# Halves of q and k brought into place by DMAs, weight loads issued from GpSimd, constants second in the queue

## The chip, the cores and the metric

The kernel runs on one core of one Trainium2 chip. The metric is the device time of one execution in microseconds (us), measured over several runs of which the median is given. Beside it stands one execution that was recorded by the hardware profiler; its span runs from the first to the last instruction. The engines are called TensorE (PE in the rows, its weight load PEld), VectorE (DVE), ScalarE (ACT), GpSimd (POOL) and SyncE (SP). The last one only issues DMAs here.

## The reference

The reference is a decoder trunk of two layers over 512 tokens of width 1024, all in float32. Each layer normalises its input, multiplies it by one wide projection, and feeds two branches:

```python
h = rmsnorm(x, norm_g)
aq, ak, av, az, bqk, bv, bi, bf, bo, bz, ga, gb = split(h @ w_in)
# (A) differential attention, 8 heads with two maps of 64 each
q = rope(rmsnorm(two_map_heads(aq), q_norm_g), cos, sin)      # the same for k
p = softmax(causal(q k^T / 8));  a = p[map 0] - lam * p[map 1]
ya = (rmsnorm(a v, attn_norm_g) * (1 - lam_init) * silu(az)) @ w_out_a
# (B) mLSTM, 8 heads, a matrix memory in stabilised form
mq, mk = split(silu(causal_conv(bqk, conv_w, conv_b)))
hb = mlstm(mq, mk, bv, bi + igate_b, bf + fgate_b)
yb = (sigmoid(bo) * rmsnorm(hb, mlstm_norm_g) * silu(bz)) @ w_out_b
x = x + (sigmoid(ga) * ya + sigmoid(gb) * yb) @ w_o
```

## The kernel before

**Precision.** TensorE is fed float32r values. A float32 operand is split in two: hi is the operand rounded to float32r (a cast), lo is the operand less hi (a subtraction). A product of two split operands takes three matmuls: hi by hi, hi by lo, lo by hi. The helper `split(hi, lo, src)` does the cast on ScalarE and the subtraction on VectorE.

**Pieces.** All weights are cut into pieces of 128 x 1024 (512 KB), 104 per layer beside the small gate piece. Each piece goes through the raw tile wr (two buffers) by a DMA, then is split into wh and wl (three buffers each), and then serves 24 matmuls of 512 columns. `TUNE["order"]` gives the order of the pieces; qk0 to qk3 are the four column groups of the attention's q and k, bqk0 to bqk7 those of the mLSTM's q and k.

**The order of the work.** The kernel's program is first recorded as a list of operations, by a class `Recorder`. Deferred steps (transposes of q and k, steps of each head) are put between the pieces at offsets given in `TUNE`. Then `schedule` plans all operations on a clock of its own, with a cost for each operation (`cost`), latencies between engines, a price per transferred byte, and waits for buffers. Each engine gets a fixed order by planned time; `issue` writes it out. On the chip every engine works through its own order and waits where an input or a buffer is late. SyncE and GpSimd have such orders too.

**q and k of the attention.** For each column group c and each tile of 128 tokens tt, `back` transposes four blocks into one PSUM tile qkt (pool tag "tr", one buffer, which the attention's transposed probabilities ut and the sums msp and den use in turn). A head pair's two maps lie in the rows 0 to 63 and 64 to 127. The destinations are 128 rows high: for q, hi in one half of the rows and lo in the other; for k, hi in both halves; for kl, lo in one half and zeros (a memset on GpSimd, `half_zero`) in the other. So one matmul with 128 rows does hi by hi and lo by hi together, and a second one hi by lo. In before, `back` fills them straight from PSUM: for each half of the rows three casts on ScalarE and two subtractions on VectorE, ten instructions of 64 x 256.

**q and k of the mLSTM.** `bqk_done` makes the convolution in y, applies silu, and fills mq, mql and mk in the same way from y: four casts and two subtractions of 64 x 512 for a q block, two and two for a k block.

**DMAs.** All DMAs are issued from SyncE: weight pieces, the rows that are spread over partitions for the mLSTM's decay (dd, em), the residual (xr, x1d), the output. `TUNE["start"]` is the order of the first loads: x0 to x3 (token tiles of the input), ng (the norm's weights), ct (constants, with the identity that transposes need), w0 and w1 (the first two weight pieces).

**Sums over partitions.** A mean of squares over the 128 rows is a matmul with ones. Unfolded, it takes hi and lo, two matmuls. For the heads in foldA, foldM and foldD the upper 64 rows are first added to the lower 64, and hi and lo are put into one tile (`fold`): one matmul.

Of the kernel before, what the change touches and what calls it, by code (L numbers as in the profile page):

```python
# [9 lines left out]
F32 = mybir.dt.float32  # L10
# [25 lines left out]

TUNE = {
    "order": (
# [4 lines left out]
    ),  # L43
    "qkt": 4,
    "gct": 15,
    "gls": 8,
    "glf": 11,
    "attn": (1, 5, 5, 9, 9, 9, 13, 16, 16, 19, 24),
    "a0": 23,
    "ap": 18,  # L50
    "a4": 8,
    "ml": (5, 9, 11, 12, 14, 28),
    "ahead": 3,
    "lc": 0,
    "slack": 4130.0,
    "margin": 200.0,
    "pemargin": 0.0,
    "wait": 308.1,
    "swpen": 11707.1,
    "smargin": 29.5,  # L60
    "pwait": 1.8,
    "wdiff": 9600.0,
    "wsp": 3,
    "kact": (0, 1, 2),
    "qsq": (1, 3),
    "foldA": (2, 3, 5, 6, 7),
    "foldM": (0, 1, 2, 3, 4, 5, 7),
    "foldD": (0, 1, 3, 4, 5, 6, 7),
    "warm": 18,
    "start": 'x0 ng w0 x1 ct w1 x2 x3',  # L70
    "gateA": 7,
    "gateM": 0,
    "actp": (2, 3),
    "m0": 218,
    "mp": 15,
    "m4": 20,
    "slots": 20,
    "bias": {'gi': 9700.0, 'ob': -1150.0, 'qkt': -1600.0, 'den': -1950.0, 'rq': -6100.0, 'gw': -3200.0, 'bo': -950.0, 'woa': -2700.0, 'mql': -2550.0, 'bz': -4700.0, 'av': 8250.0, 'msp_a': -2200.0, 'wl': -600.0, 'qk1_0x': -4100.0, 'hl': 16650.0, 'wh': -1350.0, 'qk': -2250.0, 'dd': -450.0, 'pb': -8050.0, 'ga': -1600.0, 'cv': -2050.0, 'cosv': -3250.0, 'az': -2000.0, 'ua': 3200.0, 'ang': -600.0, 'posf': -5750.0, 'gt': 10650.0, 'ut': 18200.0, 'fb_b': -200.0, 'num': -4050.0, 'sc': 26850.0, 'uh': -1250.0, 'msl_a': 3900.0, 'fb_d': -7600.0, 'rn': 5200.0, 'eps': 1400.0, 'bv': 1150.0, 'qk1_2x': -450.0, 'sinv': 3950.0, 'ks': 1650.0, 'wob': 2350.0, 'msh_d': -4100.0, 'fb_a': 2100.0, 'ul': -900.0, 'ml': -2100.0, 'gcol': -1300.0, 'ss': 6050.0, 'ms_b': -1150.0, 'ld': 8050.0, 'fo_d': 4250.0, 'em': 150.0, 'gf': -700.0, 'msl_b': -2800.0, 'kl': -250.0, 'qk0_0x': -950.0, 'xn': -150.0, 'ct': 3800.0, 'sbz': 3700.0, 'sums': 1300.0, 'rot': 6450.0, 'qss': -650.0, 'wo': -3700.0, 'lneps': 2450.0, 'hh': -2250.0, 'qt': 50.0, 'taz': 4700.0, 'par': 400.0, 'qs': 4900.0, 'fo_b': 1650.0, 'out_0_dram': -100.0, 'msl_d': -250.0, 'msp_b': 300.0, 'junk': 150.0, 'zw': -4200.0, 'mk': 1600.0, 'gft': 3600.0, 'gct': 1350.0, 'ms_a': 3750.0, 'rows': 2800.0, 'woh': -4650.0, 'warm': -3850.0, 'sbo': 500.0, 'mx': -3750.0, 'ms': 550.0, 'wr': -350.0, 'msh_b': -50.0, 'glf': 4000.0, 'bqk': 250.0, 'fo_a': 500.0, 'x': -2250.0, 'qy': 100.0, 'epsc': 1150.0, 'lq': 50.0, 'sdl': 1350.0, 'gm': 200.0},
    "drain": 173.2,
    "risk": 226.0,  # L80
    "late": 580.2,
}


# [16 lines left out]
class Recorder:  # L101
# [111 lines left out]
    @staticmethod  # L213
    def cost(eng, fn, a, k):
        def cols(ap):
            n = 1
            for x in list(ap.shape)[1:]:
                n *= x
            return n

        def ps(ap):
            return isinstance(ap, bass.AP) and ap.space == PSUM

        n = cols(a[0])
# [35 lines left out]
    def schedule(self):  # L260
# [65 lines left out]
        while len(order) < n:  # L326
# [51 lines left out]
                    load = table  # L378
            free[e] = s + c
            end[i] = s + c  # L380
            if e == "SP":
# [4 lines left out]
                dma = max(dma, s) + size / (175.0 if src.space != DRAM or src.tensor.name.startswith("rows") else 360.0)  # L386
                end[i] = max(dma, s) + 2000.0
            for t in o["tiles"]:
                r = rings[t["ring"]]
                if not t["live"]:  # L390
# [42 lines left out]
def kernel(ctx, tc, x, pos, wp, wg, cst, par, pb, ngb, out):  # L433
# [181 lines left out]
    def layer_events(l):  # L615
        lam_init = 0.8 - 0.6 * math.exp(-0.3 * l)
        par_l = pt[l]
        st = {}
# [205 lines left out]
        def qk_back(c, tt, rq):  # L824
# [8 lines left out]
            def back():  # L833
                pst = ps_tr.tile([P, 4, P], F32, tag="tr", name=f"qkt{l}_{c}_{tt}")
                for g in range(4):
                    T.transpose(pst[:, g, :], rq[:, g * P : (g + 1) * P], ident)
                ts = slice(tt * P, (tt + 1) * P)
                q0, q1, k0, k1 = (t[:, :, ts] for t in st[("qs", c)])
                kl0, kl1 = (t[:, :, ts] for t in st[("kl", c)])
# [101 lines left out]
        def bqk_done(m, acc):  # L941
# [439 lines left out]
    def load(i):  # L1381
# [2 lines left out]
        l, key = pieces[i]  # L1384
        w = wpool.tile([P, 1024], F32, tag="raw", bufs=2, name=f"wr{i}")
        if key == "gate":
            SY.dma_start(w[:, :512], wg[l])
        else:
            SY.dma_start(w, wp[l, KIDX[key]])
        loaded[i] = w  # L1390

    def prep(i):
# [131 lines left out]
```

## Time and profile before

| | |
|---|---|
| median of 3 runs (lowest to highest) | 1351.06 us (1350.99 to 1351.32) |
| the profiled execution, its span | 1351.41 us, 1349.6 us |
| TensorE busy, matmuls | 1338.7 us, 6364 |
| VectorE busy, instructions | 990.2 us, 1966 |
| ScalarE busy, instructions | 881.7 us, 1800 |
| GpSimd busy, instructions | 23.0 us, 28 |
| moved by DMAs | 137.68 MB, mean 102 GB/s |

The busy time of TensorE is modelled from pipelined matmuls, so "busy" is not the same as full use. In the rows below, a group of instructions is named by what it writes and reads, as wl<-wr,wh; then come the tile's partitions x elements, the count, the busy time and the mean ns of one, and the idle time of the engine before them with what ended it. A row of waits says who waited for whom, how long in total, how often, and the longest.

### The profile page before, as it was taken

To read this page: it belongs to the slowest core of one execution; us is meant where nothing else is said; L and a number is where in the kernel's file an instruction comes from. 1 tells how busy PE (TensorE), PEld (TensorE's weight loads), DVE (VectorE), ACT (ScalarE), POOL (GpSimd) and SP (SyncE) were. 2 spreads that over 40 slices of the span, in tenths; PEclk is the share of its full clock that TensorE was granted. 3 is DMA by queue.
4 is the path that set the end of the run, shared out by engine and by line. 5 is a ranking of instruction groups with operands and counts; after the bars stand their busy time and mean duration, and the time that the engine had idled before them with its cause. 6 is when DMAs were issued, how large, how long until landed. Compare 5 with 4: busy or idle time off the path is not lost. (4 is left out here: it accounts for less than half of the span.)

```text
span 1349.6 us, 17968 instructions
## 1 busy us (share of the span) xinstructions
PE 1338.7 (99%) x6364; PEld 1108.6 (82%) x6364; DVE 990.2 (73%) x1966; ACT 881.7 (65%) x1800; POOL 23.0 (2%) x28
## 2 busy tenths in 40 slices
PE   9999999999999999999999999999999999999998
PEld 7788888888888888888888888888888888888887
DVE  7888988785477877844568889888755778787452
ACT  6768978876356867833357788788753577677230
POOL 1000010000000000000000000000000000000000
PEclk9999999999999999999999999999999999999999
DMA  5323222323343433433622222221333534434332
GB/s 178 94 64 94 76 66 63 94 79 98 94 124 118 133 114 119 146 95 101 200 65 78 66 77 79 78 78 64 96 111 94 129 112 126 122 109 145 104 111 86
DMA packets 48394, 137.68 MB, mean 102 GB/s; under 512 B 5776, under 2 KB 12560, under 8 KB 48304
## 3 DMA queue, kind: packets, MB, share of 16 engines
q1 hardware_dynamic: 48304, 136.54, 33.2%
q8 instruction: 50, 0.82, 0.2%
q14 instruction: 40, 0.33, 0.1%
HBM read 132.25 MB, written 4.26 MB: 101 GB/s over the span
## 5 line engine op out<-in xcount | busy, mean ns | idle before, releaser
L429 DVE TENSOR_TENSOR wl<-wr,wh 128x512 fp32r<-128x512 f32 x400 | 264.7, 686 | 117.5 <-ACT wh L429 115.3
L429 ACT CAST wh<-wr 128x1024 fp32r<-128x1024 f32 (+1 forms) x202 | 210.8, 1045 | 207.1 <-PE wob L429 40.3
L429 PE MATMUL qk<-wl,hh 128*128 128x512 f32 x256 | 93.7, 402 | 0.0
L429 PE MATMUL qk<-wh,hl 128*128 128x512 f32 x256 | 93.7, 402 | 0.0
L429 PE MATMUL qk<-wh,hh 128*128 128x512 f32 x256 | 92.8, 401 | 0.2 <-ACT hh L429 0.2
L429 PE MATMUL woa<-oa,wh 128*128 128x512 f32 x256 | 87.7, 390 | 0.0
L429 PE MATMUL wob<-ob,wh 128*128 128x512 f32 x256 | 86.7, 389 | 0.0
L429 ACT ACTIVATE p<-sc,mx,rq 128x128 f32<-128x128 f32 (+3 forms) x128 | 78.6, 616 | 9.3 <-DVE mx L429 8.2
L428 ACT ACT_TABLE_LOAD x61 | 78.3, 1283 | 1.0
L429 PEld LDWEIGHTS wob<-ob,wh 128*128 128x128 f32 x256 | 47.9, 188 | 10.4 <-ACT sgb L429 0.2
L429 PEld LDWEIGHTS qk<-wl,hh 128*128 128x128 f32 x256 | 47.6, 188 | 10.4 <-DVE wl L429 0.9
L429 PEld LDWEIGHTS qk<-wh,hh 128*128 128x128 f32 x256 | 47.8, 188 | 10.0 <-ACT hh L429 0.5
L429 PEld LDWEIGHTS woa<-oa,wh 128*128 128x128 f32 x256 | 47.9, 188 | 9.6
L429 PEld LDWEIGHTS qk<-wh,hl 128*128 128x128 f32 x256 | 47.4, 188 | 9.4 <-DVE hl L429 0.4
L429 DVE TENSOR_REDUCE mx<-sc 128x2 f32<-128x256 f32 (+1 forms) x64 | 52.2, 816 | 0.4
L429 PE MATMUL bqk<-hh,wl 128*128 128x512 f32 x128 | 50.6, 395 | 0.0
L429 PE MATMUL bqk<-hl,wh 128*128 128x512 f32 x128 | 50.3, 393 | 0.0
L429 PE MATMUL bqk<-hh,wh 128*128 128x512 f32 x128 | 50.1, 392 | 0.0
L429 PE MATMUL ga<-hh,wl 128*128 128x512 f32 x128 | 49.7, 396 | 0.0
L429 PE MATMUL bo<-hh,wl 128*128 128x512 f32 x128 | 49.7, 393 | 0.0
L429 PE MATMUL ga<-hl,wh 128*128 128x512 f32 x128 | 49.4, 396 | 0.0
L429 PE MATMUL bo<-hh,wh 128*128 128x512 f32 x128 | 49.3, 393 | 0.0
(285 smaller groups left out, 3678.9 us busy)
## 6 DMA issues: line engine op xcount, KB each, us to landing
wr<-in_wp_dram SPq DMA_DIRECT2D x208, 512.0 KB, 3.5
dd<-rows SPq DMA_DIRECT2D x16, 256.0 KB, 3.9
em<-rows SPq DMA_DIRECT2D x16, 256.0 KB, 3.8
dd<-rows SPq DMA_DIRECT2D x16, 192.0 KB, 5.1
x<-in_x_dram SPq DMA_DIRECT2D x4, 512.0 KB, 4.8
dd<-rows SPq DMA_DIRECT2D x16, 128.0 KB, 6.3
xr<-in_x_dram SPq DMA_DIRECT2D x8, 256.0 KB, 4.1
x1d<-xn SPq DMA_DIRECT2D x8, 256.0 KB, 3.5
```

The lines of the kernel that those rows point to most:

```text
L428: self.tc.keep_in_program_order(self.nc.scalar.preload_act_table_set(self.SET_NAME[o["load"]]))
L429: self.tc.keep_in_program_order(getattr(o["e"], o["fn"])(*o["a"], **o["k"]))
```

## The change

The order of pieces and the numbers in `TUNE` that place and weigh operations are new throughout. The ones that change what is computed by whom are shown. `back` and `bqk_done` now split the whole 128-row block once, into two tiles h and l of the pool s2, and SyncE's DMAs bring the 64-row halves to their places: ten DMAs of 64 KB in `back`, six of 128 KB for a q block of the mLSTM and four for a k block. Weight pieces are loaded by DMAs that GpSimd issues. From the fourth piece on (`i < TUNE["wsp"]`), wl is made by one subtraction instead of two. The planner prices a DMA issue at 0.4 us on SyncE and 1 us on GpSimd, where it had 0.06 for SyncE.

```diff
-    "attn": (1, 5, 5, 9, 9, 9, 13, 16, 16, 19, 24),
+    "attn": (1, 5, 5, 8, 8, 10, 13, 16, 16, 19, 26),
-    "ahead": 3,
+    "ahead": 5,
-    "pemargin": 0.0,
+    "pemargin": 398.8,
-    "kact": (0, 1, 2),
-    "qsq": (1, 3),
-    "foldA": (2, 3, 5, 6, 7),
-    "foldM": (0, 1, 2, 3, 4, 5, 7),
-    "foldD": (0, 1, 3, 4, 5, 6, 7),
+    "kact": (0, 1),
+    "qsq": (1,),
+    "foldA": (0, 2, 3, 4, 5, 7),
+    "foldM": (0, 1, 2, 3, 4, 5, 6),
+    "foldD": (0, 1, 2, 3, 4, 5, 6, 7),
-    "start": 'x0 ng w0 x1 ct w1 x2 x3',
+    "start": 'x0 ct ng w0 x1 w1 x2 x3',
-    "actp": (2, 3),
+    "actp": (0, 3),
...
-            return 200.0 + n
+            return 1000.0 if fn == "dma_start" else 200.0 + n
...
-        return 60.0
+        return 400.0
...
+                go = s + c if e == "POOL" else s
+                dma = max(dma, go) + size / (175.0 if src.space != DRAM or src.tensor.name.startswith("rows") else 360.0)
+                end[i] = max(dma, go) + 2000.0
...
+    def halves(src, name):
+        hi, lo = t2(f"h_{name}", F32R), t2(f"l_{name}", F32R)
+        split(hi, lo, src)
+        return hi.bitcast(F32), lo.bitcast(F32)
...
+                h4, l4 = halves(pst.rearrange("p a b -> p (a b)"), f"qk{l}_{c}_{tt}")
                 for q, k, kl, a, b in ((q0, k0, kl0, L, H), (q1, k1, kl1, H, L)):
-                    A.copy(q[a], pst[a, 0:2, :])
-                    V.tensor_tensor(q[b], pst[a, 0:2, :], q[a].bitcast(F32), ALU.subtract)
-                    A.copy(k[a], pst[a, 2:4, :])
-                    A.copy(k[b], pst[a, 2:4, :])
-                    V.tensor_tensor(kl[a], pst[a, 2:4, :], k[a].bitcast(F32), ALU.subtract)
+                    SY.dma_start(q[a], h4[a, 0:2])
+                    SY.dma_start(k[a], h4[a, 2:4])
+                    SY.dma_start(k[b], h4[a, 2:4])
+                    SY.dma_start(q[b], l4[a, 0:2])
+                    SY.dma_start(kl[a], l4[a, 2:4])
...
+            hi, lo = halves(y, f"m{l}_{m}")
-                    A.copy(q[a, i, :], y[a])
-                    A.copy(q[b, i, :], y[a])
-                    V.tensor_tensor(st[("mql", grp)][i][a, pl, :], y[a], q[a, i, :].bitcast(F32), ALU.subtract)
+                    SY.dma_start(q[a, i, :].bitcast(F32), hi[a])
+                    SY.dma_start(q[b, i, :].bitcast(F32), hi[a])
+                    SY.dma_start(st[("mql", grp)][i][a, pl, :].bitcast(F32), lo[a])
...
-                    A.copy(k[a, i, :], y[a])
-                    V.tensor_tensor(k[b, i, :], y[a], k[a, i, :].bitcast(F32), ALU.subtract)
+                    SY.dma_start(k[a, i, :].bitcast(F32), hi[a])
+                    SY.dma_start(k[b, i, :].bitcast(F32), lo[a])
...
-            SY.dma_start(w, wp[l, KIDX[key]])
+            G.dma_start(w, wp[l, KIDX[key]])
...
-        if TUNE["wsp"]:
+        if i < TUNE["wsp"]:
```

More of the change, by code (lines that the diff above doesn't have):

```diff
@@ L45 @@
     "gct": 15,
-    "gls": 8,
+    "gls": 7,
     "glf": 11,
-    "attn": (1, 5, 5, 9, 9, 9, 13, 16, 16, 19, 24),
+    "attn": (1, 5, 5, 8, 8, 10, 13, 16, 16, 19, 26),
     "a0": 23,
     "ap": 18,
-    "a4": 8,
-    "ml": (5, 9, 11, 12, 14, 28),
-    "ahead": 3,
-    "lc": 0,
-    "slack": 4130.0,
-    "margin": 200.0,
-    "pemargin": 0.0,
[L58 to L62, printed above, removed]
-    "wsp": 3,
-    "kact": (0, 1, 2),
-    "qsq": (1, 3),
@@ L66 @@
-    "foldA": (2, 3, 5, 6, 7),
-    "foldM": (0, 1, 2, 3, 4, 5, 7),
-    "foldD": (0, 1, 3, 4, 5, 6, 7),
+    "a4": 4,
+    "ml": (0, 7, 10, 10, 15, 30),
+    "ahead": 5,
+    "lc": 2,
+    "slack": 11872.4,
+    "margin": 200.0,
+    "pemargin": 398.8,
+    "wait": 282.4,
+    "swpen": 421.9,
+    "smargin": 6.1,
+    "pwait": 0.1,
+    "wdiff": 2681.3,
+    "wsp": 3,
+    "kact": (0, 1),
[3 more added lines that the diff above has]
+    "foldD": (0, 1, 2, 3, 4, 5, 6, 7),
@@ L69 @@
     "warm": 18,
-    "start": 'x0 ng w0 x1 ct w1 x2 x3',
+    "start": 'x0 ct ng w0 x1 w1 x2 x3',
     "gateA": 7,
-    "gateM": 0,
-    "actp": (2, 3),
-    "m0": 218,
+    "gateM": 4,
+    "actp": (0, 3),
+    "m0": 228,
     "mp": 15,
-    "m4": 20,
+    "m4": 2,
     "slots": 20,
-    "bias": {'gi': 9700.0, 'ob': -1150.0, 'qkt': -1600.0, 'den': -1950.0, 'rq': -6100.0, 'gw': -3200.0, 'bo': -950.0, 'woa': -2700.0, 'mql': -2550.0, 'bz': -4700.0, 'av': 8250.0, 'msp_a': -2200.0, 'wl': -600.0, 'qk1_0x': -4100.0, 'hl': 16650.0, 'wh': -1350.0, 'qk': -2250.0, 'dd': -450.0, 'pb': -8050.0, 'ga': -1600.0, 'cv': -2050.0, 'cosv': -3250.0, 'az': -2000.0, 'ua': 3200.0, 'ang': -600.0, 'posf': -5750.0, 'gt': 10650.0, 'ut': 18200.0, 'fb_b': -200.0, 'num': -4050.0, 'sc': 26850.0, 'uh': -1250.0, 'msl_a': 3900.0, 'fb_d': -7600.0, 'rn': 5200.0, 'eps': 1400.0, 'bv': 1150.0, 'qk1_2x': -450.0, 'sinv': 3950.0, 'ks': 1650.0, 'wob': 2350.0, 'msh_d': -4100.0, 'fb_a': 2100.0, 'ul': -900.0, 'ml': -2100.0, 'gcol': -1300.0, 'ss': 6050.0, 'ms_b': -1150.0, 'ld': 8050.0, 'fo_d': 4250.0, 'em': 150.0, 'gf': -700.0, 'msl_b': -2800.0, 'kl': -250.0, 'qk0_0x': -950.0, 'xn': -150.0, 'ct': 3800.0, 'sbz': 3700.0, 'sums': 1300.0, 'rot': 6450.0, 'qss': -650.0, 'wo': -3700.0, 'lneps': 2450.0, 'hh': -2250.0, 'qt': 50.0, 'taz': 4700.0, 'par': 400.0, 'qs': 4900.0, 'fo_b': 1650.0, 'out_0_dram': -100.0, 'msl_d': -250.0, 'msp_b': 300.0, 'junk': 150.0, 'zw': -4200.0, 'mk': 1600.0, 'gft': 3600.0, 'gct': 1350.0, 'ms_a': 3750.0, 'rows': 2800.0, 'woh': -4650.0, 'warm': -3850.0, 'sbo': 500.0, 'mx': -3750.0, 'ms': 550.0, 'wr': -350.0, 'msh_b': -50.0, 'glf': 4000.0, 'bqk': 250.0, 'fo_a': 500.0, 'x': -2250.0, 'qy': 100.0, 'epsc': 1150.0, 'lq': 50.0, 'sdl': 1350.0, 'gm': 200.0},
@@ L79 @@
-    "drain": 173.2,
-    "risk": 226.0,
-    "late": 580.2,
+    "bias": {'sgb': -13550.0, 'den': -9800.0, 'az': 850.0, 'ut': 17100.0, 'sums': -3850.0, 'num': 15050.0, 'av': -200.0, 'warm': 6300.0, 'glf': -7950.0, 'p': 9500.0, 'ms_b': -4750.0, 'gb': -4400.0, 'bo': 2050.0, 'ld': -7050.0, 'l_m': -4650.0, 'wl': 100.0, 'msh_d': -1050.0, 'rows': 14350.0, 'mql': -8200.0, 'ms': 4750.0, 'ml': 5800.0, 'qkt': 2400.0, 'xr': -22050.0, 'fb_a': 1900.0, 'kl': 6150.0, 'sbz': -7900.0, 'gct': 13400.0, 'bz': -50.0, 'ss': 4400.0, 'ob': 8550.0, 'mk': -5450.0, 'cosv': 2500.0, 'lq': 3400.0, 'epsc': 4600.0, 'out_0_dram': 3550.0, 'sdh': 3000.0, 'taz': -1350.0, 'qss': 13250.0, 'oa': -150.0, 'rnh': -2200.0, 'fb_b': 3250.0, 'rq': -3650.0, 'cv': -350.0, 'sc': 400.0, 'msh_a': 1900.0, 'wol': 2250.0, 'gt': -750.0, 'sdl': 1750.0, 'sq': 1350.0, 'rot': -50.0, 'ks': 1600.0, 'qy': 1100.0, 'uh': -950.0, 'ul': 13150.0, 'qk1_0x': -650.0, 'eps': -1200.0, 'fo_d': -850.0, 'zeroc': -150.0, 'posf': -2200.0, 'ms_a': -500.0, 'msl_a': 1450.0, 'fb_d': -1550.0, 'em': -50.0, 'l_qk': -100.0, 'wo': -50.0, 'qk0_2x': -2000.0, 'wob': 650.0, 'mx': -1000.0, 'msh_b': 750.0, 'ng': -250.0, 'fo_a': 9300.0, 'gc': 1200.0, 'gm': 1800.0, 'qk0_0x': 1600.0, 'woa': -50.0, 'dd': 3200.0, 'zw': -150.0, 'pb': 250.0, 'lneps': -600.0, 'xn': -450.0, 'h_m': 4200.0, 'ct': -650.0, 'msp_a': -150.0, 'woh': -3000.0, 'wr': 100.0, 'hh': 1550.0, 'sinv': -100.0, 'par': 200.0, 'mq': -600.0, 'h_qk': -200.0, 'ctab': 200.0, 'ones': -1550.0},
@@ L82 @@
+    "drain": 5427.5,
+    "risk": 170.8,
+    "late": 130.5,
 }
@@ L380, in schedule @@
             end[i] = s + c
-            if e == "SP":
+            if o["fn"] == "dma_start":
                 size = 4.0
@@ L385, in schedule @@
                 src = o["a"][1]
-                dma = max(dma, s) + size / (175.0 if src.space != DRAM or src.tensor.name.startswith("rows") else 360.0)
-                end[i] = max(dma, s) + 2000.0
+                go = s + c if e == "POOL" else s
+                dma = max(dma, go) + size / (175.0 if src.space != DRAM or src.tensor.name.startswith("rows") else 360.0)
+                end[i] = max(dma, go) + 2000.0
             for t in o["tiles"]:
@@ L837, in back @@
                 ts = slice(tt * P, (tt + 1) * P)
[L838 to L839 removed]
+                h4, l4 = halves(pst.rearrange("p a b -> p (a b)"), f"qk{l}_{c}_{tt}")
+                h4, l4 = (t.rearrange("p (a b) -> p a b", a=4) for t in (h4, l4))
+                q0, q1, k0, k1 = (t[:, :, ts].bitcast(F32) for t in st[("qs", c)])
+                kl0, kl1 = (t[:, :, ts].bitcast(F32) for t in st[("kl", c)])
                 L, H = slice(0, 64), slice(64, 128)
                 for q, k, kl, a, b in ((q0, k0, kl0, L, H), (q1, k1, kl1, H, L)):
[L842 to L846 removed]
+                    SY.dma_start(q[a], h4[a, 0:2])
[3 more added lines that the diff above has]
+                    SY.dma_start(kl[a], l4[a, 2:4])
                 st[("qkn", c)] = tt + 1
```

2 lines of the change are left out of this document (1 added, 1 removed), and 8 rows, old and new, of the table TUNE.

## The prediction

> **What bounds the kernel now.** I read the page's head first, then a table of stretches, then what TensorE waited for.
>
> ```profile
> span 1349.6 us, 17968 instructions
> PE 1338.7 (99%) x6364; PEld 1108.6 (82%) x6364; DVE 990.2 (73%) x1966; ACT 881.7 (65%) x1800; POOL 23.0 (2%) x28
> PEclk9999999999999999999999999999999999999999
> ```
>
> TensorE is busy for 1338.7 of 1349.6 us at full granted clock. All that is to be won without removing matmuls is the 10.9 us between. The table of stretches shows where they are (columns: stretch, its length, busy PE, PEld, DVE, ACT, POOL, clock, DMA share, GB/s).
>
> ```profile
> 0.00:9.00 9.00, 6.16 (x19) 4.62 (x20) 3.13 (x12) 4.76 (x7) 5.89 (x10) 1.00 0.82 301
> 9.00:24.00 15.00, 14.72 (x76) 11.36 (x76) 14.01 (x40) 9.86 (x22) 0.00 (x0) 1.00 0.52 183
> 90.00:330.00 240.00, 238.14 (x1189) 197.91 (x1190) 201.37 (x456) 195.84 (x485) 4.75 (x5) 1.00 0.26 80
> 330.00:660.00 330.00, 330.00 (x1498) 274.19 (x1497) 217.84 (x337) 184.52 (x249) 2.85 (x3) 1.00 0.40 122
> 755.00:1000.00 245.00, 243.13 (x1211) 201.82 (x1211) 205.28 (x463) 200.00 (x496) 4.75 (x5) 1.00 0.25 79
> ```
>
> The first 9 us lose 2.8, the attention stages (90 to 330 and 755 to 1000) 1.9 each; 330 to 660, with the mLSTM, loses nothing. In the attention stages VectorE and ScalarE are busy 82 to 84%, so an instruction that runs later than the written-out order expects has little room to catch up. The waits of TensorE by cause (total, times, longest):
>
> ```profile
> PE msp_a L429 <- DVE fo_a L429: 1.9, 2, 0.9
> PE warm L429 <- DVE ml L429: 1.6, 1, 1.6
> PE qkt L429 <- ACT qk_2x L429: 1.5, 4, 0.5
> PE ht L429 <- DMA ct<-in_cst_dram: 1.2, 1, 1.2
> PE qkt L429 <- ACT qk_0x L429: 0.5, 1, 0.5
> PE qkt L429 <- DVE kl L429: 0.4, 2, 0.2
> PE wo L429 <- DVE xr L429: 0.3, 1, 0.3
> ```
>
> Two of these causes are touched directly: the transposes qkt wait 1.5 + 0.5 + 0.4 = 2.4 us for copies out of their PSUM tile, and the first transposes ht wait 1.2 us for the constants ct.
>
> **The change, part by part.** The copies of q and k after the transposes (32 blocks: 2 layers, 4 column groups, 4 token tiles):
>
> ```profile
> L429 ACT CAST ks<-qkt 64x256 fp32r<-64x256 f32 x64 | 23.4, 366 | 5.3 <-DVE qs L429 4.8
> L429 DVE TENSOR_TENSOR qs<-qkt,qs 64x256 fp32r<-64x256 f32 x32 | 13.5, 422 | 5.3 <-ACT qs L429 4.5
> L429 ACT CAST hh<-ht 128x512 fp32r<-128x512 f32 x16 | 9.3, 583 | 9.2 <-PE ht L429 9.1
> L429 DVE TENSOR_TENSOR hl<-ht,hh 128x512 fp32r<-128x512 f32 x16 | 10.8, 685 | 4.6 <-ACT hh L429 4.5
> ```
>
> Before, a block takes 6 casts of 0.366 = 2.20 us on ScalarE and 4 subtractions of 0.42 = 1.69 us on VectorE, all reading PSUM. After, one cast and one subtraction of 128x512 do, the shapes of hh and hl: 0.58 and 0.69 us. Over 32 blocks ScalarE loses 51.7 us of work and VectorE 32. None of that is on the path by itself: TensorE is the bound. What is on the path is the single PSUM tile of tag "tr". Before, a cast of the q half starts when its transposes are done, and the last transpose of the block waits behind that cast (the row "qkt <- ACT qk_2x"); the next user waits for all ten readers. After, no cast can start before the fourth transpose, and the tile is free after about 0.58 + 0.69 = 1.3 us of readers instead of 2.2 and more. So I take the 2.4 us off: **-2.4**. Bounds: -2.4, and 0 if another user of that tile (ut, msp_a) waits there instead.
>
> The convolved q and k of the mLSTM (16 blocks of bqk):
>
> ```profile
> L429 ACT CAST mq<-cv 64x512 fp32r<-64x512 f32 x32 | 19.8, 619 | 4.0 <-DVE cv L429 3.5
> L429 DVE TENSOR_TENSOR mk<-cv,mk 64x512 fp32r<-64x512 f32 x16 | 11.0, 686 | 3.0 <-ACT mk L429 2.5
> L429 ACT CAST uh<-sgb 128x512 fp32r<-128x512 f32 x16 | 10.0, 622 | 20.8 <-DVE sgb L429 20.8
> L429 DVE TENSOR_TENSOR wol<-wr,woh 128x1024 fp32r<-128x1024 f32 x8 | 9.8, 1224 | 9.5 <-ACT woh L429 9.5
> L429 DVE TENSOR_TENSOR wl<-wr,wh 128x512 fp32r<-128x512 f32 x400 | 264.7, 686 | 117.5 <-ACT wh L429 115.3
> ```
>
> Eight q blocks go from 4 casts to 1, eight k blocks from 2 to 1 (the shape of uh<-sgb, 0.62): 32 casts, 20 us of ScalarE; each loses one of two subtractions, 16 x 0.69 = 11 us of VectorE. From the fourth weight piece on, wl is one 128x1024 subtraction (1.22 by the row wol) for two that are busy 264.7 / 400 = 0.66 each: 0.1 us x 197 = 20 us less VectorE. Squares (qsq), key scaling (kact) and probability scaling (actp) move some further work from ScalarE to VectorE. All this lands in stages where TensorE lacks under 1% and is worth **0**; its cover is TensorE's own 99%.
>
> Matmuls: an unfolded sum over partitions takes two 512-column matmuls, a folded one takes one. foldA goes from 5 heads to 6, foldM stays at 7, foldD goes from 7 to 8: two matmuls fewer per layer, 4 in all. In the chain of work that ended last stands
>
> ```profile
> 1288.22 11.79 PE wob L429 x52
> ```
>
> so one costs 11.79 / 52 = 0.227 us: **-0.9**. This is certain.
>
> The DMAs. A block of q and k now needs 10 transfers of 64 KB from SyncE, a bqk block 6 or 4 of 128 KB: 320 + 80 = 400 more; the 208 weight loads and the 2 of the gates leave SyncE for GpSimd. Issues and landings (KB each, median us from issue to landing), the time of one issue, and what SyncE waits for:
>
> ```profile
> wr<-in_wp_dram SPq DMA_DIRECT2D x208, 512.0 KB, 3.5
> dd<-rows SPq DMA_DIRECT2D x16, 256.0 KB, 3.9
> dd<-rows SPq DMA_DIRECT2D x16, 64.0 KB, 6.7
> ct<-in_cst_dram SPq DMA_DIRECT2D x1, 212.0 KB, 6.2
> L429 SPq DMA_DIRECT2D wr<-in_wp_dram x208: 327/328/488, 1.7 to 1316.1; - x104
> L429 SPq DMA_DIRECT2D dd<-rows x64: 326/430/438, 309.8 to 1204.1; - x64
> SPq L429 <- DVE wl L429: 1092.8, 198, 13.7
> POOL kl L429 <- PE sc L429: 329.1, 2, 167.7
> ```
>
> SyncE gains 400 x 0.33 to 0.43 = 132 to 172 us of issuing and loses 210 x 0.33 = 69; it waits 1092.8 us for raw weight tiles to be freed, so there is room, and these waits leave with the weight loads (else every half would queue behind one). Behind a half that waits for its cast, the xr, rows, dd and em transfers queue. None of these shows in TensorE's waits. The bytes are 320 x 64 + 80 x 128 KB, 30.7 MB, two thirds of them in stages where the DMA share is 0.25. **0** for both, with the lateness below.
>
> The nearest row to a block's ten halves is dd: four issues, 640 KB, as much as ten halves. The fourth lands 3 x 0.43 + 6.7 = 8.0 us after the first issue. The kernel's planner (its new figures, in the diff) expects 10 issues of 0.4 and 2.0 to 2.4 more, 6.0 to 6.4 us. So a half can be up to 2 us later than planned, where before it was a ScalarE cast away. Ends: 0 (scores are placed far behind, and dd costs TensorE nothing though it lands that late) and 2 us in each of 8 column groups, +16. I take **0**, the dd row's own effect.
>
> The weights on GpSimd: what a DMA issue costs there no row shows. The nearest are its memset (4.75 us for 5 in the stretch 90 to 330, 0.95 each) and SyncE's issue, 0.33; I take 1. Cover: issue 1 + landing 3.5 + cast 1.05 + subtraction 1.2 = 6.8 us per raw tile, two of them in turn 3.4 us a piece, against 24 x 0.227 = 5.4 us of matmuls a piece. **0**; if the cover goes, the excess counts for each late piece. GpSimd also runs the 24 memsets of kl and mql in order, and before these waited up to 167.7 us for their tiles; a load behind such a memset waits too. They stand in the planner's order of time, so only its error counts.
>
> The start (start us, us, engine, operation):
>
> ```profile
> 1.63 6.09 PE L429 MATMUL warm<-zw,ones 128*128 128x512 f32 x18 [1.63 <-DVE ml L429]
> 4.32 1.06 ACT L429 ACTIVATE junk<-x 128x1024 f32<-128x1024 f32 x1 [2.29 <-DMA x<-in_x_dram]
> 6.06 1.41 DVE L429 SCALAR_TENSOR_TENSOR junk<-x,ss,ng 128x512 f32<-128x512 f32 x2 [4.44 <-ACT ss L429]
> 6.93 1.05 ACT L429 CAST wh<-wr 128x1024 fp32r<-128x1024 f32 x1 [0.90 <-DMA wr<-in_wp_dram]
> 8.22 1.06 ACT L429 ACTIVATE junk<-x 128x1024 f32<-128x1024 f32 x1 [0.24 <-DMA x<-in_x_dram]
> 8.93 1.07 PE L429 MATMUL ht<-ct,junk 128*128 128x128 f32 x8 [1.21 <-DMA ct<-in_cst_dram]
> ```
>
> x0 lands at 4.3, w0 at 6.9, x1 at 8.2: 512 KB in 1.3 us, 400 KB/us. With ct second it lands at 4.3 + 212/400 = 4.9, and ht can start when the warm-up ends at 7.72: **-1.2** at best. But w0 and w1 now run beside SyncE's transfers, not behind them. If both streams share evenly, x0 + ct + ng (1236 KB) and w0 + w1 (1024 KB), counted from 4.3 - 1.3 = 3.0, are all in at 3.0 + 2260/400 = 8.65: ng, needed by the first scaling, moves from before 6.06 to 8.65, ht to 8.65 + 0.7 + 0.1 = 9.45, half a us later than now, and x1 to 8.65 + 1.3 = 9.95, 1.75 later. The worse end is **+1.8**. I take the middle, **+0.3**: no row tells which, as all transfers of this trace run in one queue.
>
> "DMA: Bandwidth & Descriptors" of the Trainium skill, section Queues, rings and completion order, says that each DMA engine takes turns between the queues that have work. By that rule the start would be the even sharing, +0.5 to +1.8, and the sum 1.5 us higher at most; no run here shows it yet, this trace having one loaded queue.
>
> Sum: -2.4 - 0.9 + 0.3 = -3.0. The profiled execution took 1351.41 us (span 1349.6 and 1.8 around it), 0.35 over the median of 1351.06; against the median **1348.1**.
>
> **Rivals.**
> 1. No difference. The start takes the worse end (+1.8), and late halves give TensorE one wait of 2 us: -3.3 + 1.8 + 2.0 = +0.5, 1351.6; with the start alone 1349.6. For it: the gain is nearly as small as what can be told, and each new mechanism is untested in this trace. Against: VectorE and ScalarE lose some 50 and over 70 us in the stages where waits occur. (The Trainium skill's rule of turns, cited above, is this start.)
> 2. Slower: SyncE's queue delivers halves too late. TensorE's order is fixed, so a score whose half is late stops every matmul behind it. A wait of 2 us in 4 to 8 of the 8 column groups is +8 to +16 on -3.0, 1356 to 1364; I put it at 1357. It decides from 5.7 us of such waits on (3.0 + 2.7), 0.7 per group. For it: the dd row's 6.7 us. Against: scores of a tile start several pieces after its transposes, and the planner keeps 0.4 us before each matmul that reads another engine's result (pemargin), where it kept none.
> 3. Slower: weights held up on GpSimd behind a memset that waits for its tile, at about 10 us in all: 1358. For it: the 167.7 us waits. Against: raw tiles in reserve.
> 4. More: msp_a's waits (1.9) go too, with the start's best end: -2.4 - 0.9 - 1.2 - 1.9 = -6.4, 1344.7. For it: 50 to 100 us less work beside TensorE. Against: msp_a waits behind the last attention head, a chain that folding keeps.
>
> **How the numbers follow.** A difference under 0.2%, 2.7 us, can hardly be told from none. Forecast 0.32 and rival 4 0.18: faster 0.50 (1344.4 to 1348.4 is this case's own range). Rival 1: 0.31, of which 0.20 for the start alone. Rivals 2 and 3: 0.14 and 0.05, slower 0.19. The range for 8 in 10 runs from rival 4's 1344.7 to the upper part of rival 1, 1353.2; what is left out is slower than that, and a little below.
>
> **What would show it.** Right: no row of TensorE's waits with qkt and an ACT cast; qkt read by one 128x512 cast and one subtraction per block; ScalarE at 881.7 - 51.7 - 20 = 810 us or below, VectorE at 990.2 - 32 - 11 - 20 = 927 and what is moved to it; 6360 matmuls; ht starting near 7.8. Wrong: rows "sc <- DMA" or "ms <- DMA" in TensorE's waits (rival 2); "wh <- DMA wr" and POOL waits long together with idle TensorE (rival 3); ht waiting for VectorE's junk past 9 us (rival 1). The prediction fails most easily if the written-out order, which is new everywhere, runs less close to the plan than the old one: then waits stand at tiles that I did not name.

## The result, and the profile after

| | before | after |
|---|---|---|
| median (lowest to highest) | 1351.19 us (1350.99 to 1351.49) | 1393.91 us (1392.55 to 1396.33) |
| span of the profiled execution | 1349.6 us | 1390.8 us |
| TensorE busy / idle | 1338.7 / 10.9 us | 1353.0 / 37.8 us |

The change made the kernel slower: ratio 1.0318, 95% interval 1.0300 to 1.0336. The forecast was 1348.1 with a range from 1344.7 to 1353.2.

The head of the profile page of after, its packets, and the shares of the chain of work that ended last (the instructions and transfers that released each other, followed back from the last one):

```profile
span 1390.8 us, 18382 instructions
...
PE 1353.0 (97%) x6360; PEld 1116.4 (80%) x6360; DVE 946.2 (68%) x1677; ACT 798.6 (57%) x1464; POOL 134.0 (10%) x238
...
DMA packets 100749, 169.20 MB, mean 122 GB/s; under 512 B 12176, under 2 KB 59920, under 8 KB 100656
...
PE 79%; DVE 6%; DMA 5%; SPq 4%; ACT 3%; issue 2%; ACTq 0%; DVEq 0%; POOLq 0%
```

VectorE and ScalarE did lose 44 and 83 us of work. But DMAs and SyncE's queue carry 9% of the chain: work that TensorE was to hide now sets the end. (In before the chain can be followed over 26% of the span, and all of that is TensorE.) Of the 41.2 us that the span grew, 26.9 are idle time of TensorE (37.8 less 10.9) and 14.3 are longer "busy" time.

The stretches of the prediction again, in after (length, busy PE, PEld, DVE, ACT, POOL, granted clock, DMA share, GB/s):

```profile
0.00:9.00 9.00, 6.33 (x18) 4.71 (x18) 1.67 (x10) 3.98 (x6) 3.29 (x8) 1.00 0.80 295
9.00:24.00 15.00, 13.24 (x70) 10.16 (x71) 13.70 (x27) 10.57 (x22) 1.60 (x3) 1.00 0.53 186
90.00:330.00 240.00, 230.60 (x1135) 190.77 (x1134) 188.03 (x398) 163.48 (x367) 22.60 (x38) 0.98 0.40 109
330.00:660.00 330.00, 328.35 (x1492) 272.04 (x1491) 207.28 (x274) 182.78 (x249) 30.40 (x56) 1.00 0.44 126
755.00:1000.00 245.00, 236.29 (x1175) 194.93 (x1174) 200.54 (x440) 169.30 (x386) 24.51 (x40) 0.99 0.42 112
```

The attention stretches lose 9.4 and 8.7 us, where they lost 1.9 each; 330 to 660, with the mLSTM's halves in it, loses 1.7. So most of it is lost in the attention's stages. What TensorE waited for:

```profile
PE ut L430 <- DVE sums L430: 6.1, 2, 3.3
PE sc L430 <- ACT p L430: 5.0, 2, 2.6
PE msp_a L430 <- DVE l_qk L430: 4.9, 2, 2.6
PE sc L430 <- DMA kl<-l_qk: 3.5, 2, 3.2
PE qkt L430 <- DVE l_qk L430: 3.0, 4, 1.4
PE av L430 <- DVE gi L430: 2.5, 1, 2.5
```

Only one of these rows is a score that waits for its half. The others name VectorE and ScalarE, which are less busy than before. What held those two up stands in their own waits. ScalarE's and then VectorE's rows for halves:

```profile
ACT gi L430 <- DMA qk_0x<-h_qk: 11.0, 2, 7.1
...
ACT h_qk L430 <- DMA qs<-h_qk: 5.8, 2, 3.0
...
ACT h_qk L430 <- DMA ks<-h_qk: 4.8, 1, 4.8
...
ACT fb_a L430 <- DMA qs<-h_qk: 3.3, 1, 3.3
...
ACT fb_a L430 <- DMA qs<-l_qk: 3.1, 1, 3.1
```

```profile
DVE l_qk L430 <- DMA qk_2x<-h_qk: 4.3, 2, 3.6
...
DVE l_qk L430 <- DMA qk_2x<-l_qk: 3.2, 1, 3.2
...
DVE l_qk L430 <- DMA qk_0x<-h_qk: 2.1, 1, 2.1
...
DVE l_qk L430 <- DMA kl<-l_qk: 1.8, 1, 1.8
```

None of these instructions reads a half. They write into a buffer of the pool s2 (seven buffers for all of h, l, gi, fb_a and others) from which an older h or l is still being copied out. Each engine works through its written-out order, so all that stands behind such a write waits too, TensorE's inputs among it. These waits are 39.4 us in all (28.0 on ScalarE, 11.4 on VectorE). In before the readers were instructions of the engines, and none of these rows existed; here a source is held until the transfer out of it has landed.

Why the transfers are late: SyncE's issues of kl's halves (shortest, median, longest in ns), beside those of xr, and the landings.

```profile
L430 SPq DMA_DIRECT2D kl<-l_qk x64: 590/606/1545, 46.0 to 950.6; - x64
```

```profile
L430 SPq DMA_DIRECT2D xr<-in_x_dram x8: 327/328/414, 586.8 to 672.3; - x8
```

```profile
kl<-l_qk SPq DMA_DIRECT2D x64, 64.0 KB, 3.2
...
qk_0x<-h_qk SPq DMA_DIRECT2D x48, 64.0 KB, 3.6
...
ct<-in_cst_dram SPq DMA_DIRECT2D x1, 212.0 KB, 3.8
```

One issue of a half takes 0.60 us, not 0.33 to 0.43, and with the pause behind it SyncE issues one in 0.65 us. The 40 of the first column group go out from 43.3 to 72.4 us with few pauses; at the planner's 0.4 they would take 16 us. Compared one by one with the plan's times, the first of the group starts 0.6 us late and the last 13.3. The same comparison gives 30.5 us at the end of layer 0's fourth group, 32.1 at the start of layer 1's first, and 59.3 at the end of the last: nearly the whole delay against the plan arises in the stages with the attention's transfers, and 1.6 us in the stage between. The piece of the chain of work in the first group (start, length, what):

```profile
43.32 5.33 DMA qk_0x<-h_qk
...
51.31 2.59 DMA qk_0x<-h_qk
53.90 0.68 DVE l_qk L430
...
54.63 0.66 PE qkt L430 x4
...
62.88 4.63 DMA qk_0x<-l_qk
...
67.67 1.31 PE sc L430 x3
```

First a transfer out of an old tile ends (53.90), then the subtraction that was to write there runs, then the next transposes (54.63); 13 us later a score waits for its half. Four-microsecond stretches around that wait, TensorE alone (length, busy and matmuls, granted clock, DMA share, GB/s):

```profile
62.00:66.00 4.00, 1.54 (x8) 1.00 1.07 256
66.00:70.00 4.00, 2.74 (x7) 0.65 0.33 76
70.00:74.00 4.00, 4.00 (x19) 0.92 0.52 100
```

After the gap the clock falls. The trace's clock record has seven stretches of 3.41 us at half clock in after, at 67.2, 128.7, 179.9, 251.6, 746.5, 818.2 and 937.6 us, each behind a gap of 2.3 to 3.3 us; before has none until its last instruction. By estimate such a stretch costs half its length, 1.7 us; seven of them are 12 of the 14.3 us of longer busy time.

### The profile page after: what moved, and what is told of

Read it like the earlier page. It is cut to its first block, busy times and chain, and to the rows that moved or that the text cites. A ratio compares the mean times of both kernels' runs of the same rounds, so it can differ in the third digit from the quotient of the medians.

```text
span 1390.8 us, 18382 instructions
## 1 busy us (share of the span) xinstructions
PE 1353.0 (97%) x6360; PEld 1116.4 (80%) x6360; DVE 946.2 (68%) x1677; ACT 798.6 (57%) x1464; POOL 134.0 (10%) x238
## 4 chain that ended last, share of the span: by engine, by line
PE 79%; DVE 6%; DMA 5%; SPq 4%; ACT 3%; issue 2%; ACTq 0%; DVEq 0%; POOLq 0%
PE qk L430 11%; PE bv L430 6%; PE wo L430 6%; PE wob L430 6%; PE bz L430 6%; PE woa L430 6%; PE ga L430 6%; PE gb L430 6%; PE bqk L430 5%; PE bo L430 5%; SPq L430 4%; PE av L430 4%; PE sc L430 2%; PE az L430 2%; PE num L430 2%
## 5 line engine op out<-in xcount | busy, mean ns | idle before, releaser
L430 DVE TENSOR_TENSOR wl<-wr,wh 128x1024 fp32r<-128x1024 f32 (+1 forms) x203 | 244.8, 1207 | 91.0 <-ACT wh L430 89.7
L430 POOL DMA_DIRECT2D wr<-in_wp_dram x208 | 110.0, 529 | 1217.2 <-DVE wl L430 873.8
L430 PE MATMUL woa<-oa,wh 128*128 128x512 f32 x256 | 92.3, 390 | 0.0
L430 PE MATMUL az<-hh,wh 128*128 128x512 f32 x128 | 51.0, 404 | 0.0
L430 PE MATMUL av<-wh,hh 128*128 128x512 f32 x128 | 48.4, 416 | 2.5 <-DVE gi L430 2.5
L430 PE MATMUL az<-hh,wl 128*128 128x512 f32 x128 | 50.6, 400 | 0.0
L430 PE MATMUL az<-hl,wh 128*128 128x512 f32 x128 | 50.5, 400 | 0.0
```

What stands on the lines that cost most here:

```text
L430: self.tc.keep_in_program_order(getattr(o["e"], o["fn"])(*o["a"], **o["k"]))
```

## The experiments

On the planner's own clock before ends at 1330.1 us, and the chip at 1349.6: 19.5 us later. After ends there at 1330.7, and the chip 60.1 later. This distance between planned end and measured span is the measure in what follows, because each variant of the code gets another plan:

| kernel | plan ends | span | distance | median time |
|---|---|---|---|---|
| before | 1330.1 | 1349.6 | 19.5 | 1351.2 |
| e3, weights from GpSimd alone | 1342.7 | 1364.1 | 21.4 | 1363.7 |
| e8, new numbers alone | 1355.4 | 1376.0 | 20.6 | 1376.0 |
| e6, attention by copies | 1362.8 | 1383.9 | 21.1 | 1386.3 |
| after | 1330.7 | 1390.8 | 60.1 | 1393.9 |
| e7, mLSTM by copies | 1330.7 | 1396.4 | 65.7 | 1393.1 |
| e1, l transfers from GpSimd | 1330.7 | 1386.4 | 55.7 | 1386.2 |
| e2, issue priced | 1343.4 | 1388.9 | 45.5 | 1391.5 |
| e5, issue and landing priced | 1350.3 | 1393.1 | 42.8 | 1394.9 |
| e9, as after, planned buffers | 1330.7 | 1389.6 | 58.9 | 1391.8 |
| e10, as e2, planned buffers | 1343.4 | 1373.2 | 29.8 | 1374.9 |
| e11, as e5, planned buffers | 1350.3 | 1374.1 | 23.8 | 1375.0 |
| e13, as e11, order searched anew | 1330.1 | 1356.2 | 26.1 | 1357.6 |
| e14, as e13, buffers not fixed | 1330.1 | 1370.4 | 40.3 | 1372.5 |
| e15, as e13, two weights from SyncE | 1329.3 | 1354.7 | 25.4 | 1357.8 |

The span is that of the one profiled execution. For e7 that is the slowest of its four; by its median the distance would be about 61.

### Which part of the change: e3, e4, e6, e7, e8

e3 is before with the weight loads, and nothing else, from GpSimd (and the planner's new prices for DMAs):

```diff
...
-            SY.dma_start(w, wp[l, KIDX[key]])
+            G.dma_start(w, wp[l, KIDX[key]])
```

> The kernel before with one part of the change: weight loads issued from GpSimd, with the new prices and the new handling of GpSimd's transfers in the planner, halves made by ScalarE and VectorE as before. The planner's own clock ends at 1342.7, since its numbers were tuned for other prices. Theory: weight loads from GpSimd cost nothing beyond the plan: 1342.7 + 19.5 + 1.8 = 1364 within 5. Rival 1 (weight loads come late): the distance to the plan grows to the changed kernel's 60 us, 1404. Rivals 2 and 3 say 1364 too.

1363.73 us, at the distance of before. The weights are not late (rival 3 of the prediction falls); that e3 is slower than before lies in its plan, whose numbers were not found for it.

e4 is before with the start's order alone changed:

```diff
-    "start": 'x0 ng w0 x1 ct w1 x2 x3',
+    "start": 'x0 ct ng w0 x1 w1 x2 x3',
```

> The kernel before with the constants second in the queue, nothing else; all transfers stay in SyncE's one queue. Theory: ct lands before the warm-up ends, ht starts near 7.8 us instead of 8.93, up to 1.2 us gained: 1350.0 within 1. Rival: ng and w0 come 0.5 us later and the first scaling waits for ng: 1351 to 1352, no gain.

1352.01 us, ratio 1.0008 (0.9998 to 1.0017). No difference, as the rival said: constants that come earlier gain nothing.

e6 is after with the attention's `back` of before, e7 after with the mLSTM's copies of before, e8 before with all of after's `TUNE` and none of its code:

```diff
-                    SY.dma_start(q[a], h4[a, 0:2])
+                    A.copy(q[a], pst[a, 0:2, :])
...
```

> The changed kernel, in which the attention's q and k are filled by casts and subtractions from PSUM as in before; the mLSTM's halves still come by DMA, weights from GpSimd, the new order's numbers kept. The plan ends at 1362.8 us, later than that of the changed kernel (1330.7), because the numbers were not found for this work. Theory (the attention's 320 transfers make the distance of 60 us between plan and chip): it falls back to about 20, 1362.8 + 20 + 1.8 = 1385, 1380 to 1390, and the attention's stretches hold no wait for a DMA. Rival A (the new order or something else in it makes the distance): 1362.8 + 60 = 1423.

> The changed kernel, in which the mLSTM's q and k are filled by casts and subtractions as in before; the attention's halves still come by DMA. The plan ends at 1330.7 us, as that of the changed kernel. Theory (the loss is in the attention's column groups, 64 KB transfers ten to a block): 1388 to 1394, as the changed kernel. Rival B (the 80 transfers of 128 KB of the mLSTM are late as well and carry part of it): 1375 to 1385.

> The kernel before with all numbers of the change (order of the pieces, offsets, weights of the planner, folds), and none of its code: q and k by copies, weights from SyncE. The plan ends at 1355.4 us. Theory (an order that was planned with right durations is followed): 1355.4 + 20 + 1.8 = 1377, 1373 to 1381. Rival A (the new order itself runs badly on the chip, with small reserves between engines): 1390 or more.

e6 1386.30, e7 1393.12, e8 1376.00 us: all three as the theory said. The order by itself is followed (20.6), the order with the attention's halves is not (60.1), and without them it is again (21.1). In time e6 is only 7.6 us below after, because its own plan is 32 us longer; that the loss comes with the attention's 320 transfers rests on the distances and on the delays counted above. The mLSTM's 80 add nothing that e7 shows: its time is that of after, with the same planned end.

### Pace, price, or something else: e1, e2, e5

e1 keeps after's order and issues the transfers out of l tiles from GpSimd, so that SyncE has six to a block and not ten:

```diff
+            e = o["e"]
+            if o["fn"] == "dma_start" and o["a"][1].tensor.name.startswith("l_"):
+                e = self.nc.gpsimd
...
```

> The changed kernel with the planner's order untouched: only when the program is written out, the transfers that read an l tile (4 of the 10 of a block, 2 of the 6 or 4 of a bqk block) are issued from GpSimd instead of SyncE. Theory (SyncE's issue: 0.6 us and more each where the planner counts 0.4): a block then costs SyncE 6 x 0.645 = 3.9 us, planned 4.0, so the queue keeps up; at least 30 of the 42.7 us come back, 1352 to 1364. Rival 1 (weight loads from GpSimd come late): GpSimd gets still more to issue, 1394 or slower. Rival 2 (the new order is bad in itself): same order, 1394 within 4. Rival 3 (the transfers land late because they are many and small, wherever issued): 1390 to 1398.

1386.21 us, 7.7 less than after. A miss for the theory, and outside what each rival said: taking four of ten issues off SyncE gives little back. But landings got longer at the same time: in e1 that of kl is 4.6 us at the median and of qk_0x 5.4. So this run does not separate SyncE's pace from late landings.

e2 prices a half's issue at 0.65 us in the planner, e5 also its landing at 4.0 us:

```diff
-        return 400.0
+        return 650.0 if a[0].shape[0] == 64 else 400.0
...
-                end[i] = max(dma, go) + 2000.0
+                end[i] = max(dma, go) + (4000.0 if o["a"][0].shape[0] == 64 else 2000.0)
```

> The changed kernel with one figure of the planner changed: a transfer to 64 rows issued from SyncE is priced 0.65 us, not 0.4. The planner's own clock then ends 12.7 us later than for the changed kernel (1343.4 against 1330.7; for the kernel before it ended at 1330.1, and the chip took 1349.6, 19.5 more). Theory (SyncE's issue): the chip follows the plan again, 20 to 30 us above it: 1365 to 1375 with the 1.8 us around the span. Rivals 1 to 3 (weight loads, the order, small transfers): the distance to the plan stays at the changed kernel's 60 us, 1403 or so.

> The changed kernel, in which the planner prices what the traces showed of a half: 0.65 us of issuing (it had 0.4) and 4.0 us from issue to landing (it had 2.0). The planned order alone changes; on the planner's own clock it ends at 1350.3 us. Before ends at 1330.1 there and at 1349.6 on the chip, 19.5 later; the changed kernel at 1330.7 and 1390.8, 60 later; with the issue alone priced, 1343.4 and 1388.9, 45.5 later. Theory (the halves, and with them the tiles that they are read from, come free later than the order assumes, and the engines that wait for them stop TensorE): with the landing in the plan the chip follows it again, 1350.3 + 20 + 1.8 = 1372, 1368 to 1378. Rival A (the lateness is something that the prices of halves don't hold, the order of the pieces or clock dips): the distance stays at 40 to 45, 1392 to 1397.

1391.46 and 1394.91 us. The theory misses both, and e5 is where its rival A said: a truer price makes the planned end later by 12.7 and 19.6 us, and the chip stays where it was. So part of the distance comes from something that no price of a half holds.

### The buffers: e9 to e12

That something stands in the compiled programs. The planner gives a new tile the buffer of s2 that comes free first in time. The code that hands the buffers out has a rule of its own. The order in which the last readers are issued explains all 329 reuses in before and most of the 425 in after; what decides the others is open. For a tile whose last reader is a copy the two orders are almost the same. For a tile whose last reader is a transfer, the issue is early and the end late. By the addresses of the compiled programs, 8 of 336 tiles of s2 lie elsewhere than planned in before (behind another tile than the plan has there), 62 of 432 in after, 94 in e2, 134 in e5. In after, gi is planned into the buffer of rot, long free, and lies in that of h_qk: the row "gi <- DMA qk_0x<-h_qk: 11.0" above. e9 (after), e10 (e2), e11 (e5) and e12 (before) write the planner's own choice out, and change nothing else:

```diff
+SLOT = {
+    "s2": (
...
+            if self.n in SLOT:
+                t = self.p.tile(shape, dt, tag=f"{tag}_{SLOT[self.n][self.k]}", bufs=1, name=name)
...
```

> The changed kernel with the same planned order; only which of the seven buffers of pool s2 a tile gets is written out, as the planner assumed it. In the changed kernel 62 of 432 tiles of that pool lie in another buffer than planned (in the program text: gi waits there for the six transfers out of h_qk, where the plan gives it a buffer that was long free); in before 8 of 336, in the kernel with attention copies 32 of 368. Theory S (buffers are handed out in the order of their last readers, which takes no note of when a transfer ends, so tiles are made to wait for transfers that the plan had kept clear of them, and the engine behind them stands): the waits of ScalarE and VectorE for halves, 39.4 us, shrink to below 20, and the time falls to 1370 to 1386. Rival I (SyncE's pace alone makes the tiles late, whichever they are): 1390 to 1395.

> As the kernel that prices a half's issue at 0.65 us (plan 1343.4; measured 1391.5, span 1388.9), with the planned buffers of s2 written out; there 94 of 432 tiles lay elsewhere. Theory S: the chip follows the plan, 1343.4 + 20 + 1.8 = 1365, and up to 8 more where landings are later than the plan's 2.0 us: 1363 to 1374. Rival I: no change, 1388 to 1393.

> As the kernel that prices issue and landing (0.65 and 4.0 us; plan 1350.3; measured 1394.9), with the planned buffers of s2 written out; there 134 of 432 tiles lay elsewhere. Theory S: 1350.3 + 20 + 1.8 = 1372, 1368 to 1376, and TensorE idle near the plan's. Rival I (something else that no price holds): 1390 to 1396.

> The kernel before with the planned buffers of s2 written out; 8 of 336 tiles lay elsewhere, none read by a DMA out of turn. Both theories: no change, 1349.5 to 1352.

e10 1374.93 (0.9 over its range), e11 1375.01 us: 16.5 and 19.9 less than e2 and e5 by the buffers alone, and e11 is 23.8 from its plan. e12 is 1350.72, ratio 0.9997 (0.9988 to 1.0007). e9 misses: 1391.77, and its waits for halves stay at 34.8 us. In e9's plan a half is still priced at 0.4 and 2.0, so each h and l comes free later than planned whatever buffer it lies in; its last half starts 58.9 us behind the plan, that of e11 20.5. Neither cause alone gives more than 2.5 us back. The two together give 19 of the 42.7, and bring the chip to 23.8 us from its plan. Pricing the landing too (e11 beside e10) makes the plan 7 us longer and the distance 6 shorter; the time stays the same.

ScalarE's waits for halves in e11:

```profile
ACT taz L441 <- DMA ks<-h_qk: 2.8, 2, 1.4
ACT taz L441 <- DMA kl<-l_qk: 2.8, 1, 2.8
...
ACT taz L441 <- DMA qk_2x<-h_qk: 1.8, 1, 1.8
...
ACT h_qk L441 <- DMA qk_0x<-h_qk: 0.4, 1, 0.4
```

7.8 us, where after has 28.0; no gi and no fb_a among them. VectorE's fall from 11.4 to 3.7.

### What is left: e13 to e15

e11's plan ends 20 us later than before's, with numbers that were found under the wrong prices. For e13 they were searched anew under the true ones, on the planner's clock only, until its end came back to 1330.1 us; e14 is e13 without the written-out buffers (152 of 432 lie elsewhere).

> The changed kernel, planned anew: a half is priced at 0.65 us of issue and 4.0 us to landing, the planned buffers of s2 are written out (as in the run at 1375.0), and the order's numbers were searched again under these prices, until the plan ends at 1330.1 us, where before's ends too. Theory O (what is left over before at 1375.0, 24 us, is an order found for wrong prices: 1350.3 against 1330.1 on the planner's clock): 1330.1 + 20 to 24 + 1.8 = 1352 to 1357, with its excess over before in the first 24 us and in small waits. Rival D (400 transfers more cost time by themselves, by what they do to weight loads and to the engines beside them): 1363 or more.

> The same order with its honest prices, but the buffers of s2 handed out as in the changed kernel, in the order of their last readers: 152 of 432 tiles lie elsewhere than planned. Theory S (slots): 12 to 25 us over the run with planned buffers, 1365 to 1380, with new waits of ScalarE and VectorE for halves. Rival (slots matter little where the prices are right): within 3 us of it.

e13 1357.62 us, ratio 1.0055 (1.0038 to 1.0072), just over its upper end; e14 1372.49, 14.9 more by the buffers alone. Stretches of e13 (columns as above), then ScalarE's rows for halves in e14:

```profile
0.00:9.00 9.00, 5.80 (x18) 4.38 (x18) 0.75 (x8) 3.95 (x6) 3.30 (x8) 1.00 0.75 289
9.00:24.00 15.00, 13.07 (x62) 9.89 (x63) 13.46 (x28) 9.88 (x22) 1.06 (x2) 0.89 0.50 172
24.00:330.00 306.00, 304.71 (x1516) 252.91 (x1516) 254.55 (x550) 211.84 (x475) 33.89 (x56) 1.00 0.47 124
330.00:730.00 400.00, 396.54 (x1809) 327.12 (x1808) 244.59 (x347) 205.88 (x311) 37.28 (x69) 1.00 0.43 124
730.00:1040.00 310.00, 310.00 (x1532) 258.19 (x1531) 238.34 (x488) 202.54 (x435) 34.50 (x57) 1.00 0.46 123
1040.00:1346.00 306.00, 303.98 (x1387) 251.97 (x1386) 189.34 (x255) 161.97 (x219) 25.05 (x48) 1.00 0.44 122
```

```profile
ACT gi L425 <- DMA qk_0x<-h_qk: 10.9, 2, 6.7
...
ACT h_qk L425 <- DMA ks<-h_qk: 5.7, 2, 3.5
...
ACT h_qk L425 <- DMA qs<-l_qk: 4.3, 2, 3.1
```

With all 320 transfers in place, TensorE is idle for 1.3 of 306 and 0 of 310 us in the attention stages of e13. So the transfers by themselves leave no idle time of TensorE there, where the plan makes room for them. What e13 still loses lies at the start (5.1 of 24 us, with the clock at 0.89; before loses 3.1) and in the mLSTM's stages (3.5 of the 400 us of layer 0's, and 2.0 of the last 306).

Of the 42.7 us that the change cost, true prices and planned buffers together gave 19 back (e11), the order that was searched anew under them 17.4 more (e13), and 6.4 stay.

e15 is e13 with the first two weight pieces put back into SyncE's queue, behind ct and ng (planned again, with its own planned buffers):

```diff
-            G.dma_start(w, wp[l, KIDX[key]])
+            (SY if i < 2 else G).dma_start(w, wp[l, KIDX[key]])
```

> As the replanned kernel with planned buffers (1357.6), with the first two weight pieces issued from SyncE in the order of the start (x0, ct, ng, w0, x1, w1), so that they queue behind ct and ng there; all later pieces from GpSimd. The plan ends at 1329.3 us (1330.1). Theory P (weights beside the start's other transfers delay x0, ct and ng together; ht starts at 10.5 us there and at 8.9 in before, and the gap is followed by 3.4 us at half clock): ht starts before 9, the dip goes, 2 to 4 us less, 1353.5 to 1355.5. Rival (the order of the start's transfers, not the second queue): ht as late, no change, 1356.5 to 1358.5.

```profile
8.16 0.60 PE L436 MATMUL ht<-ct,junk 128*128 128x128 f32 x4
...
10.38 0.49 PE L436 MATMUL qk<-wh,hh 128*128 128x512 f32 x1 [0.72 <-ACT wh L436]
```

ht starts at 8.16 and not at 10.52, and the dip of the clock at 11.5 us is gone, as expected; but the median is 1357.78 us, no less, as the rival said. The theory's reason is not shown either. The first work on x0 starts at 4.62 us in e13 and at 4.59 in e15, so x0 was not late. What changed as well is VectorE's order: in e13 the subtraction of the first weight piece (9.06) stands ahead of the scaling that ht reads (9.67), in e15 the scaling comes first (6.87). The profiled execution is 1.5 us shorter than e13's, and one dip of 3.41 us stands at 1171.5 us, behind a gap of 2.1 at den; e13 has a gap of 2.0 there and no dip. So the rest of 6.4 us over before stays open: the start and the mLSTM's gaps before den are where the traces show it, and no run has taken the second away. No version here beats before.

## Why the prediction was wrong

**The step that failed** is "The DMAs", which put 0 for SyncE's issues and 0 for late halves, with an upper end of +16. Rival 2 named the right queue and was given 0.14, but its path, a score that waits for its half, is only 4.0 us of TensorE's waits (rows "sc <- DMA"). Four things in the step were wrong.

- The price of an issue. It was taken from rows of transfers between DRAM and SBUF (0.33 to 0.43). The issue of a 64-row half from SBUF to SBUF takes 0.60 us, and the next one goes out after 0.65. No row of before had that shape, and 0.43 stood as the upper end.
- The queue. Lateness was worked out for one block of ten issues: up to 2 us. Four blocks of a group follow each other in 16 planned us, so what SyncE falls behind adds up: 13.3 us at the end of the first group.
- Who waits. The step asked when a score gets its half. It didn't ask when the source gets free: two tiles of seven per block, held until the last of up to six transfers out of them has landed. That is where 39.4 us of ScalarE's and VectorE's waits come from. The prediction had read that in the attention stages a late instruction "has little room to catch up", but gave it no term.
- The buffers. That an order planned for one set of buffers runs on another could not be seen in the trace of before, where 8 of 336 tiles lie elsewhere and none of them behind a tile that a transfer reads last. The prediction's last sentence, that it fails most easily if the order "runs less close to the plan than the old one", is what happened. It stood there without a term or a chance; the distance of 60.1 us, against 19.5, is its size.

On top came, by the estimate above, 12 us of half clock that no term had. The price of a gap was its length; in after seven of eight gaps of 2.3 to 3.3 us cost some 1.7 more. "TensorE: Matmul & The Clock Gate" of the Trainium skill, section "What's actually happening", says that the clock falls to one half after about 3.4 us without work, judged in free-running windows of 3.41 us. The traces agree on the half and on the 3.41 us. But shorter gaps could be enough here, from 2.1 us on (e15), though not each: one of 2.8 in after brought no dip.

**What held.** A block's cast and subtraction take 0.581 and 0.689 us (0.583 and 0.685 were said), TensorE does 6360 matmuls, and ScalarE is at 798.6 us (810 or below). Weights from GpSimd cost nothing later on (e3); the issue takes 0.53 us there, not 1. The term of -2.4 did not hold: the row "qkt <- ACT" is gone, but "qkt <- DVE l_qk", 3.0 us, stands in its place, because that subtraction now waits for its buffer. The -0.9 for four matmuls can't be told from the rest in these runs.

**The start** was put at +0.3. Busy time of TensorE in the first 24 us falls from 20.9 to 19.6, so it cost about 1.3, inside the bound of +1.8. ht starts at 9.52 us, close to the 9.45 of the even sharing, but that is luck, for it came by another path (start, length, what in after):

```profile
6.98 1.05 ACT L430 CAST wh<-wr 128x1024 fp32r<-128x1024 f32 x1 [0.81 <-DMA wr<-in_wp_dram]
8.06 0.69 DVE L430 TENSOR_TENSOR wl<-wr,wh 128x512 fp32r<-128x512 f32 x1 [6.43 <-ACT wh L430]
8.67 1.41 DVE L430 SCALAR_TENSOR_TENSOR junk<-x,ss,ng 128x512 f32<-128x512 f32 x2
```

x0 is worked on from 4.46 us, as in before (4.32), and ct has landed at 5.0. But the written-out order of VectorE has the subtraction of the first weight piece, which waits for w0 and its cast, ahead of the scaling (junk) that ht reads; in before the scaling starts at 6.06. A wait of ht for junk past 9 us is the sign that the prediction gave for rival 1. "DMA: Bandwidth & Descriptors" of the Trainium skill (Queues, rings and completion order) says that each DMA engine takes turns between the queues that have work. These traces don't settle it for the start: w0 from a queue of its own is there by 6.98 us in after and by 7.99 in e13, against 8.13 in e4, which has the same order in one queue, and the landing of ng is not in the trace.

**The gain** was worth nothing from the start: 127 us of work taken off two engines that were not the bound. The sum had this right, and no run shows a gain from it; it should have set the scale for the risk on the other side.

## What to carry to other kernels

When a copy is replaced by a transfer, ask not only when its result arrives but how long its source stays held, and who is to write there next: the wait shows up on an engine that has nothing to do with the transfer. Price an issue from a row of the same kind (here SBUF to SBUF, 64 rows), multiply by all that queue behind each other, and not by one block. Where an order is planned ahead, compare its own end with the measured span: a distance that grows tells that the plan's prices or its buffers are not those of the chip, and here both had to be put right before either showed.

## What was not expected of the hardware

- An issue on SyncE took 0.60 us for halves of 64 KB from SBUF to SBUF (median of kl in after), 0.54 to 0.59 for halves of 128 KB (medians of mql and mq), and 0.33 for a load from DRAM (xr).
- A half of 64 KB landed 2.0 us after its issue at best and 6.9 at most in after; of the attention's 160 recorded landings one in ten took over 5.0.
- Seven of the eight gaps of TensorE of 1.8 us and more in after were followed by 3.41 us at half clock; one of 2.8 us was not. Gaps of 3.9 to 4.7 us in e1 were followed by 6.8 us, and so was one of 2.9 in e3.
